# Recurrence outputs in PSUM tiles of their own, the block inverse issued a wave later, and row maxima turned by one product and one transfer

## The chip, the core and the metric

The kernel runs on one core of a Trainium2 chip. The metric is the time of one execution on the device in microseconds (us). Five engines work side by side, each through its own queue in a fixed order: TensorE (PE; its weight loads are shown apart as PEld), VectorE (DVE), ScalarE (ACT), GpSimd (POOL) and SyncE (SP, which here only issues DMAs).

## The reference

Two layers (`DEPTH = 2`) of a diffusion backbone over 256 context and 1024 latent tokens, model width 1024. Each layer scales and shifts the stream, makes one wide input projection, and feeds three groups of heads:

- A: six heads of 64 of a bidirectional recurrence (RWKV-7). Each head keeps a 64 x 64 state `S`; forward and backward scans run over context, then latent tokens.
- B: six query heads over two key heads, softmax attention over all keys.
- C: four heads of neighbourhood attention, 8 x 16 windows with a bias, plus all context keys.

Their gated outputs go through one output projection and a layer norm. The recurrence and the softmax are what the change touches:

```python
def _rwkv7_step(S, inp):
    r, w, k, v, kk, b = inp
    sa = jnp.einsum('bhvk,bhk->bhv', S, kk)
    S = S * w[:, :, None, :] - sa[..., None] * b[:, :, None, :] + v[..., None] * k[:, :, None, :]
    return S, jnp.einsum('bhvk,bhk->bhv', S, r)
...
        s = jnp.einsum('bqgrd,bsgd->bgrqs', qi, keys).astype(jnp.float32)
        p = jax.nn.softmax(s, axis=-1).astype(vals.dtype)
        return jnp.einsum('bgrqs,bsgd->bqgrd', p, vals)
```

## The kernel before

The program is written as tile code in Python; a scheduler that models the engines' times orders each engine's instructions when the program is built, taking the ready instruction that was written earliest. On the chip the order of each engine is then fixed: an instruction that waits holds up all that stand behind it on its engine.

**Layers.** A layer is `layer_proj` (projections, weights and activations split in a high and a low part, three products each, L203 to L205), `rwkv` (the recurrence, called in the middle of the projections by `mid()`), `attention` and `out_proj`. The recurrence is written ahead of the attention, so its instructions come first where both are ready, and attention fills what is left. Both overlap from 575 to 1160 us in layer 0 and from 1800 to 2385 us in layer 1; these two stretches are called the mixed stretches below.

**Recurrence.** 1280 tokens are cut into ten waves of 128, a wave into four steps of 32 tokens; the three head pairs and both directions of a step are computed together. `wave_chain` (L681 on) does a step: twelve products `rs` (L704) of the state with the keys; ACT copies them to `rsb` (L710); twelve products `sa` (L715) with the inverse block `tt`; ACT (three) and DVE (one) copy them into the state tile `x` (L721); twelve products `z` (L725) make the new state, which DVE scales into the next `x` (L730). The step's output, `out_step` (L742 to L744), is twelve products into `y`, which DVE copies to `yst`; it is put on the list `pend` and written into the next step, between `rs` and `rsb`. `rs`, `sa`, `z` and `y` are columns of one PSUM bank, the tile `ch`: `rs` and `sa` have columns 0 to 191, `z` 0 to 383, `y` 320 to 511. Only three state tiles `X` are there, so step s + 3 writes over the one that the output of step s reads.

**Preparation.** Each wave is prepared ahead by six stages: `p` (`wave_pre`: load, decay; it ends with `dc`, a copy of the decays on DVE, L575), `g` (`wave_gram`: products `gt` masked into `G`), `l` (`wave_low`: the diagonal blocks go out to `ls_d` in DRAM and come back turned as `lin`, L595 to L601), `i` (`wave_inv`: two DVE copies of `lin` to `nn`, L635 and L636, then 30 small DVE steps, and a round through DRAM to `di`), `k` (`wave_kt`: transposes), `m` (`wave_merge`: 192 small products `mg`, L675, that make `tt`). The small PSUM products of preparation (`psz`, `pcu`, `gt`, `kt`, `mg`, and `pso` of `out_block`) share two slots of the pool `pa`, tag `pp`. The main loop (L790 to L799) orders the stages of an iteration as `kpglmi`, so `i` of a wave is written right behind its `l`, ahead of the next wave's chain.

**Attention.** The heads are cut into 30 units (each of the ten heads has one for latent queries in each layer, and one for context queries in layer 0). A unit has two jobs of up to 512 queries. `pair_max` (L856) computes the scores a first time (`sm`, L867) and takes each query's maximum on DVE (L869 to L871; then `nm`, L874, one column of 128 queries). Each column is then turned into a row by a product with the identity (`mt`, L880, 180 of them, two PE instructions each), and ACT copies a job's row into row 64 of the query tile `q[1]` (L881). `pair_main` computes the scores again, turned (`st`: L936, and L937 which has row 64 among its 65 rows and so subtracts the maximum), exponentiates (ACT, L943) and multiplies with the values (L921). The maxima of a unit are interleaved with the main part of the unit before; the count `npc` in `attention` (L1076) paces them.

Of the kernel before, what the change touches and what calls it, by code (L numbers as in the profile page):

```python
# [8 lines left out]
F32 = mybir.dt.float32  # L9
# [34 lines left out]
def body(tc, a):  # L44
# [467 lines left out]
    def rwkv(l, lay):  # L512
# [10 lines left out]
        y = bank[:, 320:512].rearrange("p (c v) -> p c v", c=3)  # L523
# [22 lines left out]
        def wave_pre(w):  # L546
            dc = r2.tile([128, 2, 4, 3], F32, tag="dc", name="dc", bufs=4)
            prep[w] = dict(dc=dc, d=[], g=[])
            for d in range(2):
# [25 lines left out]
                nc.vector.tensor_copy(dc[:, d], lp[:, :, :, 32 * o:32 * o + 1].rearrange("p c j o -> p (j o) c"))  # L575
# [107 lines left out]
        def wave_chain(w):  # L683
# [5 lines left out]
            for j in range(4):  # L689
# [10 lines left out]
                for c in range(3):  # L700
                    for d in range(2):
                        for p in range(2):
                            q = QSA[d][p]
                            nc.tensor.matmul(out=rs[q:q + 32, c, :], lhsT=gs[d][:, jc[d], c, p, 0:32], rhs=x[:, d, c, p, :],  # L704
                                             start=True, stop=True, tile_position=(0, q))
                for f in pend:
                    f()
                pend.clear()
                rsb = r2.tile([128, 3, 64], F32, tag="rsb", name="rsb")
                nc.scalar.copy(rsb, rs)  # L710
# [26 lines left out]
        def out_step(w, j, x, jc, gs, yst):  # L737
            for c in range(3):
                for d in range(2):
                    for p in range(2):  # L740
                        q = QSA[d][p]
                        nc.tensor.matmul(out=y[q:q + 32, c, :], lhsT=gs[d][:, jc[d], c, p, 32:64], rhs=x[:, d, c, p, :],  # L742
                                         start=True, stop=True, tile_position=(0, q))
            nc.vector.tensor_copy(yst[:, j], y)  # L744
            if j == 3:
                for d in range(2):
                    for p in range(2):
                        q = QSA[d][p]
                        nc.sync.dma_start(out=y_d[d, 128 * w:128 * w + 128, :][:, 192 * p:192 * p + 192].rearrange("(j t) f -> t j f", t=32),
                                          in_=yst[q:q + 32].rearrange("t j c v -> t j (c v)"))  # L750
# [39 lines left out]
        for w in range(-3, NW):  # L790
            if w >= 0:
                wave_chain(w)
            for c in "kpglmi":
                v = w + (2 if c in "km" else 3)
# [13 lines left out]
    def attention(l):  # L808
# [47 lines left out]
        def pair_max(q, k, jobs, nq, bias):  # L856

            nm = ap2.tile([128, 8], F32, tag="nm", name="nm")
            for i, job in enumerate(jobs):
                q0 = job["q0"]  # L860
                for qt in range(nq // 128):
                    qc = q0 + 128 * qt
                    pcs = job["parts"](qt)
                    mx = ap2.tile([128, 4], F32, tag="mx", name="mx", bufs=4)
                    for n_, (c0, o, bcol) in enumerate(pcs):
                        sp_ = pst.tile([128, 512], F32, tag="sm", name="sm", bufs=2)
                        nc.tensor.matmul(out=sp_[:, :o], lhsT=q[0][:, qc:qc + 128], rhs=k[0][:, c0:c0 + o], start=True, stop=True)  # L867
                        if bcol is None:
                            nc.vector.tensor_reduce(out=mx[:, n_:n_ + 1], in_=sp_[:, :o], op=ALU.max, axis=AX.X)  # L869
                        else:  # L870
                            nc.vector.tensor_tensor_reduce(out=sp_[:, :o], in0=sp_[:, :o], in1=bias[0][:, bcol:bcol + o], scale=1.0, scalar=-3.0e38,  # L871
                                                           op0=ALU.add, op1=ALU.max, accum_out=mx[:, n_:n_ + 1])
                        if n_ == len(pcs) - 1:
                            nc.vector.tensor_reduce(out=nm[:, 4 * i + qt:4 * i + qt + 1], in_=mx[:, :len(pcs)], op=ALU.max, axis=AX.X, negate=True)  # L874
                        yield
            for i, job in enumerate(jobs):
                q0 = job["q0"]
                mt = pst.tile([128, 512], F32, tag="sm", name="mt", bufs=2)
                for qt in range(nq // 128):
                    nc.tensor.matmul(out=mt[64:65, 128 * qt:128 * qt + 128], lhsT=nm[:, 4 * i + qt:4 * i + qt + 1], rhs=ident, start=True, stop=True, tile_position=(0, 64))  # L880
                nc.scalar.copy(q[1][64:65, q0:q0 + nq], mt[64:65, :nq])  # L881
                yield
# [186 lines left out]
        while True:  # L1069
# [3 lines left out]
            if nxt is not None:  # L1073
                q, k, v, jobs, nq, och, bias = nxt
                mg = pair_max(q, k, jobs, nq, bias)
                npc = sum(len(j["parts"](t)) for j in jobs for t in range(nq // 128)) + 2  # L1076
# [315 lines left out]
```

## Time and profile before

| | |
|---|---|
| median of 3 runs | 2510.26 us (2495.68 to 2519.41) |
| the profiled execution's own time | 2503.84 us |
| its span, first to last instruction | 2502.0 us |
| granted TensorE clock over the span | 0.926 |
| busy: PE, DVE, ACT, POOL | 88%, 66%, 39%, 47% of the span |
| mixed stretch of layer 0 | 575 to 1160 us |
| mixed stretch of layer 1 | 1800 to 2385 us |

A row of the grouped instructions reads: line, engine, operation, output and inputs, shapes, count | busy time and mean duration | idle time of that engine just before them and what ended it. In the list of waits a row says who waited for whom, the total, how often and the longest. A row of the timeline has the start, the time until the last of the merged instructions ends, and the engine.

### The profile page before, as it was taken

The numbers are of one execution on the slowest core, as the hardware profiler recorded it, in microseconds if no ns is written. First come the engines' busy times: TensorE is split into PE (matmuls) and PEld (weight loads), VectorE is DVE, ScalarE is ACT, GpSimd is POOL, SyncE is SP. The second block draws the span as 40 slices with busy tenths as digits, with TensorE's granted clock in tenths as the row PEclk, the third lists the DMA queues.
The fourth block names the chain that finished last, engine by engine and source line by source line (L and its number), as shares of the span: only waits on it lengthen the run. The fifth ranks groups of instructions, "written<-read, shape, count | busy, mean of one in ns | idle before, by whom it ended". The sixth has DMA issues, their size and how long they took to land.

```text
span 2502.0 us, 57786 instructions
## 1 busy us (share of the span) xinstructions
PE 2204.5 (88%) x22616; PEld 1655.1 (66%) x22616; DVE 1660.7 (66%) x3183; ACT 978.7 (39%) x2074; POOL 1188.3 (47%) x1438
## 2 busy tenths in 40 slices
PE   6989999986878798999899999999868788989897
PEld 4777898764555555555797777787655555645497
DVE  5686524546887778676386795524478787777746
ACT  3333413333544344554234434223334434445522
POOL 3464426335564454453246356334456545545443
PEclk9999999997898899989999999999869989989899
DMA  7345335446555434452332455335555444432332
GB/s 278 111 158 167 109 92 127 114 108 142 120 123 115 109 93 106 125 156 60 99 100 90 138 166 184 104 88 130 143 113 126 92 105 107 96 81 66 122 113 93
DMA packets 448241, 298.17 MB, mean 119 GB/s; under 512 B 249600, under 2 KB 395880, under 8 KB 446944
## 3 DMA queue, kind: packets, MB, share of 16 engines
q1 hardware_dynamic: 439936, 281.71, 41.2%
q0 software_dynamic: 7392, 10.28, 1.5%
q8 instruction: 178, 2.92, 0.5%
q10 hardware_dynamic: 640, 2.49, 0.4%
q14 instruction: 95, 0.78, 0.1%
HBM read 198.37 MB, written 91.79 MB: 116 GB/s over the span
## 4 chain that ended last, share of the span: by engine, by line
PE 47%; DVE 21%; DMA 14%; issue 6%; ACT 5%; SPq 4%; POOL 3%; DVEq 0%; POOLq 0%; ACTq 0%
PE pj L203 5%; PE pj L204 5%; PE pj L205 5%; PE y L921 4%; DMA ls_d<-G 3%; PE sm L867 2%; PE st L936 2%; DVE mx L869 2%; DVE e L646 2%; DMA lin<-ls_d 2%; PE pj L1159 2%; PE st L937 2%; DVE G L616 2%; PE pj L1161 2%; PE pj L1160 2%
## 5 line engine op out<-in xcount | busy, mean ns | idle before, releaser
L204 PE MATMUL pj<-hlo,wh 128*128 128x512 f32 (+1 forms) x1072 | 403.0, 376 | 12.3 <-DVE hlo L480 7.2
L203 PE MATMUL pj<-hhi,wh 128*128 128x512 f32 (+1 forms) x1072 | 404.9, 380 | 7.4 <-ACT qr L348 4.7
L205 PE MATMUL pj<-hhi,wl 128*128 128x512 f32 (+1 forms) x1072 | 400.8, 375 | 0.0
L204 PEld LDWEIGHTS pj<-hlo,wh 128*128 128x128 f32 x1072 | 205.6, 192 | 54.9 <-DVE hlo L480 7.3
L169 POOL TENSOR_TENSOR wl<-wf,wh 128x512 fp32r<-128x512 f32 x104 | 142.2, 1371 | 209.3 <-ACT wh L168 194.6
L203 PEld LDWEIGHTS pj<-hhi,wh 128*128 128x128 f32 x1072 | 205.0, 192 | 52.8 <-issue 7.0
L943 ACT ACTIVATE pt<-st 128x512 f32<-128x512 f32 (+1 forms) x292 | 165.2, 582 | 174.7 <-PE st L937 171.4
L205 PEld LDWEIGHTS pj<-hhi,wl 128*128 128x128 f32 x1072 | 205.5, 192 | 37.7 <-issue 3.1
L869 DVE TENSOR_REDUCE mx<-sm 128x1 f32<-128x512 f32 (+1 forms) x372 | 198.9, 553 | 39.2 <-PE sm L867 37.5
L921 PE MATMUL y<-pt,v 128*64 128x256 f32 (+1 forms) x1392 | 221.2, 406 | 2.7 <-ACT pt L943 2.3
L936 PE MATMUL st<-q,k 128*128 128x512 f32 (+3 forms) x376 | 168.0, 451 | 22.6 <-DVE am L110 6.5
L867 PE MATMUL sm<-k,q 128*128 128x256 f32 (+2 forms) x436 | 169.7, 432 | 19.5 <-DVE mx L869 7.8
L1159 PE MATMUL pj<-yh,wh 128*128 128x256 f32 x576 | 160.0, 294 | 11.8 <-ACT yh L1133 10.7
L1160 PE MATMUL pj<-yl,wh 128*128 128x256 f32 x576 | 164.7, 289 | 0.8 <-POOL yl L1134 0.8
L1161 PE MATMUL pj<-yh,wl 128*128 128x256 f32 x576 | 163.2, 288 | 0.0
L921 PEld LDWEIGHTS y<-pt,v 128*64 128x64 f32 x1392 | 97.1, 146 | 96.3 <-issue 66.3
L950 POOL TENSOR_TENSOR acc<-acc,pt 128x512 f32<-128x512 f32 x80 | 104.5, 1306 | 116.5 <-ACT pt L943 109.9
L937 PE MATMUL st<-q,k 65*128 65x512 f32 (+3 forms) x376 | 151.3, 406 | 1.4 <-ACT q L881 1.3
L867 PEld LDWEIGHTS sm<-k,q 128*128 128x128 f32 x436 | 84.8, 210 | 81.6 <-issue 21.0
L616 DVE TENSOR_TENSOR G<-gt,msk 64x192 f32<-64x192 f32 (+1 forms) x320 | 110.5, 345 | 39.6 <-PE gt L611 28.7
L699 POOL MEMSET X<- 32x192 f32 x320 | 82.9, 259 | 93.2 <-PE ch L742 68.8
L630 ACT COPY S<-kt 64x192 f32<-64x192 f32 x320 | 100.4, 314 | 55.4 <-PE ch L725 28.7
(276 smaller groups left out, 5137.2 us busy)
## 6 DMA issues: line engine op xcount, KB each, us to landing
wf<-win SPq DMA_DIRECT2D x104, 256.0 KB
wm<-wmod SPq DMA_DIRECT2D x32, 512.0 KB
yf<-yg_d SPq DMA_DIRECT2D x72, 128.0 KB
wt<-wm SPq DMA_DIRECT2D x8, 1024.0 KB
gate_d<-o SPq DMA_DIRECT2D x32, 256.0 KB
wf<-wout SPq DMA_DIRECT2D x16, 512.0 KB
ldkk<-rw_d SPq DMA_DIRECT2D x40, 192.0 KB
ldkd<-rw_d SPq DMA_DIRECT2D x40, 192.0 KB
```

The costliest lines, as they stand in the source:

```text
L203: nc.tensor.matmul(out=ps[:, :n], lhsT=wh, rhs=hhi[:, k, t0:t0 + n], start=(k == 0), stop=False)
L204: nc.tensor.matmul(out=ps[:, :n], lhsT=wh, rhs=hlo[:, k, t0:t0 + n], start=False, stop=False)
L205: nc.tensor.matmul(out=ps[:, :n], lhsT=wl, rhs=hhi[:, k, t0:t0 + n], start=False, stop=(k == KT - 1))
L867: nc.tensor.matmul(out=sp_[:, :o], lhsT=q[0][:, qc:qc + 128], rhs=k[0][:, c0:c0 + o], start=True, stop=True)
L869: nc.vector.tensor_reduce(out=mx[:, n_:n_ + 1], in_=sp_[:, :o], op=ALU.max, axis=AX.X)
L921: mm = nc.tensor.matmul(out=y[64 * i:64 * i + 64, a0:a1], lhsT=v[:, t, :], rhs=pt[:, p0:p0 + a1 - a0], start=start, stop=stop and at == le ...
L936: nc.tensor.matmul(out=o, lhsT=k[0][:, 128 * t:128 * t + 128], rhs=q[0][:, qa:qb], start=True, stop=False)
L937: mm = nc.tensor.matmul(out=o, lhsT=k[1][0:65, 128 * t:128 * t + 128], rhs=q[1][0:65, qa:qb], start=False, stop=True)
L943: nc.scalar.activation(out=pt[:, :w], in_=sp_[:, :w], func=AF.Exp)
L1159: nc.tensor.matmul(out=p_, lhsT=wh[m][:, k], rhs=yh, start=(x_ == 0), stop=False)
L1160: nc.tensor.matmul(out=p_, lhsT=wh[m][:, k], rhs=yl, start=False, stop=False)
L1161: nc.tensor.matmul(out=p_, lhsT=wl[m][:, k], rhs=yh, start=False, stop=(x_ == KT - 1))
```

## The change

Four edits:

1. `out_step` takes its output from a tile `py` of the pool `pa` (tag `pp`) and no longer from a strip of the bank `ch`; ACT and not DVE copies it to `yst`; and `rsb` is written ahead of the outputs that are on the list `pend`.
2. The copy `dc` goes from DVE to ACT.
3. The stages of an iteration stand as `ikpglm`, and `i` works on the wave w + 2 where it worked on w + 3: the inverse of a wave is written one iteration later than its `l`, ahead of the other stages of that iteration.
4. The maxima of a whole unit are reduced at once (`nm`, 8 columns or 2), turned by one product to 8 rows of 128 (`mt`), copied by ACT to `mr`, and flattened by a DMA that POOL issues into row 64 of `q[1]`; the separate reductions, the 180 products and the 60 copies go. `npc` is one less.

```diff
-        y = bank[:, 320:512].rearrange("p (c v) -> p c v", c=3)
...
-                nc.vector.tensor_copy(dc[:, d], lp[:, :, :, 32 * o:32 * o + 1].rearrange("p c j o -> p (j o) c"))
+                nc.scalar.copy(dc[:, d], lp[:, :, :, 32 * o:32 * o + 1].rearrange("p c j o -> p (j o) c"))
...
+                rsb = r2.tile([128, 3, 64], F32, tag="rsb", name="rsb")
+                nc.scalar.copy(rsb, rs)
                 for f in pend:
                     f()
                 pend.clear()
-                rsb = r2.tile([128, 3, 64], F32, tag="rsb", name="rsb")
-                nc.scalar.copy(rsb, rs)
...
         def out_step(w, j, x, jc, gs, yst):
+            y = pa.tile([128, 3, 64], F32, tag="pp", name="py")
...
-            nc.vector.tensor_copy(yst[:, j], y)
+            nc.scalar.copy(yst[:, j], y)
...
-            for c in "kpglmi":
-                v = w + (2 if c in "km" else 3)
+            for c in "ikpglm":
+                v = w + (2 if c in "ikm" else 3)
...
-                        if n_ == len(pcs) - 1:
-                            nc.vector.tensor_reduce(out=nm[:, 4 * i + qt:4 * i + qt + 1], in_=mx[:, :len(pcs)], op=ALU.max, axis=AX.X, negate=True)
                         yield
-            for i, job in enumerate(jobs):
-                q0 = job["q0"]
-                mt = pst.tile([128, 512], F32, tag="sm", name="mt", bufs=2)
-                for qt in range(nq // 128):
-                    nc.tensor.matmul(out=mt[64:65, 128 * qt:128 * qt + 128], lhsT=nm[:, 4 * i + qt:4 * i + qt + 1], rhs=ident, start=True, stop=True, tile_position=(0, 64))
-                nc.scalar.copy(q[1][64:65, q0:q0 + nq], mt[64:65, :nq])
-                yield
+            nc.vector.tensor_reduce(out=nm[:, :n], in_=mx[:, :n, :len(pcs)], op=ALU.max, axis=AX.X, negate=True)
+            mt = pst.tile([128, 512], F32, tag="sm", name="mt", bufs=2)
+            nc.tensor.matmul(out=mt[:n, 0:128], lhsT=nm[:, :n], rhs=ident, start=True, stop=True)
+            mr = ap2.tile([8, 128], F32R, tag="mr", name="mr")
+            nc.scalar.copy(mr[:n], mt[:n, 0:128])
+            q0 = jobs[0]["q0"]
+            nc.gpsimd.dma_start(out=q[1][64:65, q0:q0 + 128 * n].rearrange("o (n t) -> o n t", t=128), in_=mr[:n])
+            yield
...
-                npc = sum(len(j["parts"](t)) for j in jobs for t in range(nq // 128)) + 2
+                npc = sum(len(j["parts"](t)) for j in jobs for t in range(nq // 128)) + 1
```

The scheduler orders the whole program anew. Two places show it.

The first is PE in layer 1, at the fourth neighbourhood unit and the fifth wave of the recurrence (wave 4, counted from 0). Before, the turning products `mt` stand in lots of seven and one (each product is two PE instructions), and the `st` product that reads row 64 (L937) stands two rows behind the first lot; `ch` with `tt` is `sa`, with `S` it is `z`, and `pcu` is preparation.

```order
7629 L867 MATMUL sm<-k_24678,q_24686 128x256
7630 L880 MATMUL mt<-c_ident,nm 1x128 x7
7631 L568 MATMUL pcu<-tri,th 128x128 x3
7632 L937 MATMUL st<-q_24687,k_24679 128x512
7633 L725 MATMUL ch<-X_17549,S_17536 64x64 x6
7634 L725 MATMUL ch<-X_17549,S_17537 64x64 x6
7635 L880 MATMUL mt<-c_ident,nm 1x128
```

In the changed program, one product `mt`, and behind it outputs `py` of two steps, then the `rs` (L703) and `sa` (L714) of a step, and only then the first L938, which reads row 64.

```order
7692 L878 MATMUL mt<-c_ident,nm 8x128
7693 L937 MATMUL st<-q_24455,k_24447 128x512
7694 L742 MATMUL py<-X_17350,G_17332 32x64 x2
...
7700 L742 MATMUL py<-X_17348,G_17332 32x64 x2
...
7706 L937 MATMUL st<-q_24455,k_24447 128x512
7707 L703 MATMUL ch<-X_17349,G_17332 32x64 x2
...
7713 L714 MATMUL ch<-rsb,tt 32x64 x12
7714 L938 MATMUL st<-q_24456,k_24448 128x512 x2
```

Seven products went, and the reader of row 64 moved from two rows behind the turning product to behind 24 outputs, two `st` products and a step's `rs` and `sa`.

The outputs moved too. Before, the output of a step (here the one in X_17549) stands right behind the `rs` of the next (X_17550):

```order
7646 L704 MATMUL ch<-X_17550,G_17532 32x64 x2
7647 L704 MATMUL ch<-X_17550,G_17533 32x64 x2
7648 L742 MATMUL ch<-X_17549,G_17532 32x64 x2
7649 L742 MATMUL ch<-X_17549,G_17533 32x64 x2
```

In the changed program, for the same wave, the output of its first step (X_17349) stands behind the second lot of merge products of the next wave:

```order
7680 L922 MATMUL y<-pt_24608,v 64x128
7681 L674 MATMUL mg<-di 32x32 x48
7682 L742 MATMUL py<-X_17349,G_17332 32x64 x2
7683 L742 MATMUL py<-X_17349,G_17333 32x64 x2
```

So an output waits for a slot that preparation holds: those of the first three steps of this wave (X_17349, X_17350, X_17348) stand in one lot, and the fourth step, which writes over X_17349 (row 7707), stands behind them.

The second place is DVE in layer 1, at the two copies `nn<-lin` that start the inverse of the sixth wave. Before, the first stands two rows behind a step's new state (L730) and ahead of the masking of `gt` (L616); the second comes eleven rows later (row 1918).

```order
1905 L730 TENSOR_TENSOR X_17550<-ch,dc 64x6x64 x2
1906 L955 TENSOR_TENSOR acc_24469<-acc_24469,pt_24625 128x256
1907 L635 COPY nn<-lin 64x256
1908 L955 TENSOR_TENSOR acc_24468<-acc_24468,pt_24625 128x128
1909 L744 COPY yst<-ch 128x192
1910 L616 TENSOR_TENSOR G_17535<-gt,msk 64x3x64 x8
```

In the changed program, for the same wave, the first stands seven rows behind the new state of the same step (L729) and behind that masking (L615); the second is row 1713.

```order
1693 L729 TENSOR_TENSOR X_17350<-ch,dc 64x6x64 x2
1694 L873 ISA sm,mx<-sm,bs 128x384
1695 L873 ISA mx 128x1
1696 L871 TENSOR_REDUCE mx<-sm 128x1
1697 L1003 TENSOR_TENSOR gtl<-ys,tb 128x4x16x8
1698 L615 TENSOR_TENSOR G_17335<-gt,msk 64x3x64 x8
1699 L946 TENSOR_TENSOR pt_24347<-st,bt 128x384
1700 L634 COPY nn<-lin 64x256
```

The start of the inverse has moved by a few rows within the same step, not by a wave, and the copy `yst` is no longer among DVE's rows.

More of the change, by code (lines that the diff above doesn't have):

```diff
@@ L858, in pair_max @@
             nm = ap2.tile([128, 8], F32, tag="nm", name="nm")
+            n = 2 * nq // 128
+            mx = ap2.tile([128, 8, 3], F32, tag="mx", name="mx")
             for i, job in enumerate(jobs):
@@ L863, in pair_max @@
                     pcs = job["parts"](qt)
-                    mx = ap2.tile([128, 4], F32, tag="mx", name="mx", bufs=4)
+                    u = nq // 128 * i + qt
                     for n_, (c0, o, bcol) in enumerate(pcs):
@@ L868, in pair_max @@
                         if bcol is None:
-                            nc.vector.tensor_reduce(out=mx[:, n_:n_ + 1], in_=sp_[:, :o], op=ALU.max, axis=AX.X)
+                            nc.vector.tensor_reduce(out=mx[:, u, n_:n_ + 1], in_=sp_[:, :o], op=ALU.max, axis=AX.X)
                         else:
                             nc.vector.tensor_tensor_reduce(out=sp_[:, :o], in0=sp_[:, :o], in1=bias[0][:, bcol:bcol + o], scale=1.0, scalar=-3.0e38,
-                                                           op0=ALU.add, op1=ALU.max, accum_out=mx[:, n_:n_ + 1])
-                        if n_ == len(pcs) - 1:
-                            nc.vector.tensor_reduce(out=nm[:, 4 * i + qt:4 * i + qt + 1], in_=mx[:, :len(pcs)], op=ALU.max, axis=AX.X, negate=True)
+                                                           op0=ALU.add, op1=ALU.max, accum_out=mx[:, u, n_:n_ + 1])
                         yield
-            for i, job in enumerate(jobs):
-                q0 = job["q0"]
-                mt = pst.tile([128, 512], F32, tag="sm", name="mt", bufs=2)
-                for qt in range(nq // 128):
-                    nc.tensor.matmul(out=mt[64:65, 128 * qt:128 * qt + 128], lhsT=nm[:, 4 * i + qt:4 * i + qt + 1], rhs=ident, start=True, stop=True, tile_position=(0, 64))
-                nc.scalar.copy(q[1][64:65, q0:q0 + nq], mt[64:65, :nq])
-                yield
+            nc.vector.tensor_reduce(out=nm[:, :n], in_=mx[:, :n, :len(pcs)], op=ALU.max, axis=AX.X, negate=True)
[6 more added lines that the diff above has]
+            yield
         def pair_main(q, k, v, jobs, nq, och, bias, end):
```

## Prediction

> **What bounds the kernel now.** I read the page's totals first, then the windows by stage, then the list of waits of PE.
>
> ```profile
> span 2502.0 us, 57786 instructions
> ...
> PE 2204.5 (88%) x22616; PEld 1655.1 (66%) x22616; DVE 1660.7 (66%) x3183; ACT 978.7 (39%) x2074; POOL 1188.3 (47%) x1438
> ...
> PE 47%; DVE 21%; DMA 14%; issue 6%; ACT 5%; SPq 4%; POOL 3%; DVEq 0%; POOLq 0%; ACTq 0%
> ```
>
> PE is busy 88% of the span and has the largest share of the chain that ended last; DVE is next, with 21% (525 us). The two mixed stretches, where recurrence and attention share the engines, hold all that the change touches, but for the first waves' preparation:
>
> ```profile
> core 0: us, PE busy (x) PEld busy (x) DVE busy (x) ACT busy (x) POOL busy (x), PEclk, DMA share, GB/s
> 575.00:1160.00 585.00, 494.55 (x7098) 317.59 (x7097) 450.15 (x1118) 273.50 (x645) 304.41 (x379) 0.88 0.47 117
> 1800.00:2385.00 585.00, 488.70 (x7017) 317.35 (x7017) 457.16 (x1080) 268.98 (x608) 310.40 (x390) 0.87 0.44 106
> sum 1170.00, PE 983.25 PEld 634.95 DVE 907.32 ACT 542.48 POOL 614.81; mean PE 491.62 PEld 317.47 DVE 453.66 ACT 271.24 POOL 307.41
> ```
>
> In 1170 us PE is busy 983 and idle 187; DVE is busy 907 (78%), ACT only 542. What PE waits for in its idle time:
>
> ```profile
> PE kt L626 <- DVE tt L680: 20.2, 9, 5.1
> PE ch L725 <- DVE X L721: 19.1, 10, 4.5
> PE ch L715 <- ACT rsb L710: 17.2, 9, 5.3
> PE mg L675 <- DVE di L678: 10.6, 3, 7.9
> PE mt L880 <- DVE mx L869: 9.9, 6, 7.3
> PE pcu L568 <- DVE th L565: 9.2, 7, 3.0
> ...
> PE mg L675 <- issue: 7.1, 7, 2.2
> ```
>
> The releaser is mostly DVE: PE's work and DVE's lateness set the mixed stretches. A recurrence step shows how:
>
> ```profile
> 910.66 0.54 PE L704 MATMUL ch<-X,G 128*32 128x64 f32 x24
> ...
> 911.02 0.52 PE L742 MATMUL ch<-X,G 128*32 128x64 f32 x24
> ...
> 911.87 1.29 DVE L869 TENSOR_REDUCE mx<-sm 128x1 f32<-128x512 f32 x2
> ...
> 913.07 0.35 DVE L744 COPY yst<-ch 128x192 f32<-128x192 f32 x1
> ...
> 913.51 0.32 ACT L710 COPY rsb<-ch 128x192 f32<-128x192 f32 x1 [0.25 <-DVE yst L744]
> ```
>
> `rs` is done at 911.20, but ACT copies it at 913.51: the copy waits for `yst` on DVE, and that one stood behind two maxima. A step loses 2.3 us here. The groups that the terms below use:
>
> ```profile
> L880 PE MATMUL mt<-c_ident,nm 128*1 128x128 f32 x360 | 56.7, 300 | 17.8 <-DVE mx L869 9.9 <-DVE mx L871 6.0 <-DVE nm L874 1.9
> ...
> L715 PE MATMUL ch<-rsb,tt 32*32 32x64 f32 x1920 | 51.6, 238 | 18.7 <-ACT rsb L710 18.4
> ...
> L575 DVE COPY dc<-lp 128x12 f32<-128x12 f32 x40 | 28.5, 711 | 56.8 <-ACT lp L573 56.6
> ...
> L881 ACT CAST q<-mt 1x512 fp32r<-1x512 f32 (+1 forms) x60 | 27.7, 470 | 26.4 <-PE mt L880 25.8
> ...
> L874 DVE TENSOR_REDUCE nm<-mx 128x1 f32<-128x3 f32 (+2 forms) x180 | 26.5, 147 | 2.0
> L710 ACT COPY rsb<-ch 128x192 f32<-128x192 f32 x80 | 25.5, 319 | 106.8 <-DVE yst L744 94.3 <-PE ch L704 5.8 <-DVE G L616 2.3
> L744 DVE COPY yst<-ch 128x192 f32<-128x192 f32 x72 | 25.3, 351 | 16.9 <-PE ch L742 15.7 <-DMA stg<-q_d 0.5
> ...
> L636 DVE COPY nn<-lin 64x256 f32<-64x256 f32 x20 | 9.4, 469 | 73.5 <-DMA lin<-ls_d 73.4
> ```
>
> **The change part by part.**
>
> *Products of the maxima (A, B).* 180 products of two PE instructions become 30, so 300 instructions go. What one costs in PE's stream:
>
> ```profile
> 928.60 0.82 PE L880 MATMUL mt<-c_ident,nm 128*1 128x128 f32 x6
> 929.35 0.66 PE L996 MATMUL tb<-c_ident,rb 128*128 128x128 f32 x4
> ...
> 935.99 0.38 PE L880 MATMUL mt<-c_ident,nm 128*1 128x128 f32 x2
> 936.30 0.50 PE L867 MATMUL sm<-k,q 128*128 128x512 f32 x1
> ```
>
> Six take 0.75 us until the next instruction starts (0.125 each), a lone pair 0.31 (0.155). 300 x 0.125 to 0.155 is 37 to 46 us; I take 42 (0.14). It lies on the engine that is the bound: A = -42. Ahead of these products PE sat idle 17.8 us, since they come as soon as the last maximum may be there; thirty products in place of sixty lots leave half: B = -9, from 0 to -18.
>
> *DVE's work (C).* `yst` (25.3) and `dc` (28.5, much of it spent blocked, as 12 elements a row need no 711 ns) leave DVE, and 150 of 180 small reductions (26.5 x 150/180 = 22.1): 76 us, 4.6% of DVE's 1661. The chain has 525 us of DVE; 4.6% of that is C = -24. It ends at 0 if other rows stand ready to take its place on the chain, at -76 if each microsecond passes through. ACT takes over 72 `yst` at the 0.32 of `rsb`, the same shape (23 us), and 40 `dc` at no more than that (13), and gives back most of the 27.7 of the 60 casts. ACT is idle 628 us of 1170 in the mixed stretches, so this is taken at nothing; without that cover it would be some 15 us.
>
> *`rsb` ahead of the outputs (D).* ACT was idle 94.3 us for `yst` ahead of `rsb`, but PE itself sat idle only 18.4 of it ahead of `sa`, since attention filled the rest. D = -12, from 0 to -18. What is late next is the copy of `sa` by DVE (L721), in the list above with 19.1.
>
> *Outputs in slots of `pa`.* The order of PE (the change, above) shows that the output now stands behind `mg` of the next wave, and the fourth step behind the lot of outputs. The products are the same in number, and attention stands ahead in that gap, so I take nothing; the upper bound is what PE already waits for preparation in the list (`kt` 20.2, `mg` 10.6 and 7.1, `pcu` 9.2), paid once more: +47.
>
> *The inverse a wave later.* DVE stood 73.4 us for `lin`, 3.7 a wave. The order shows the start of the inverse moved by a few rows in the same step, so the wait for `lin` can stay; all of it gone would be worth at most its share of the chain, 73.4 x 21% = 15. On the other side the merge now follows its inverse's own round through DRAM within an iteration; the nearest price is that same 73.4. The order leaves two to three steps between the two, so I take nothing, from -15 to +73.
>
> *The flattening transfer (E).* New in each unit: between the cast and the first L938 lies a DMA that POOL issues. The only POOL transfers inside the mixed stretches are `zs`; POOL's queue also holds the sums of the exponentials:
>
> ```profile
> zs<-zs_d POOLq DMA_DIRECT2D x40, 49.0 KB, 2.3
> ```
> ```profile
> L950 POOL TENSOR_TENSOR acc<-acc,pt 128x512 f32<-128x512 f32 x80 | 104.5, 1306 | 116.5 <-ACT pt L943 109.9 <-PE ch L742 3.9 <-DVE mx L869 1.9
> ```
>
> Issue to landing takes 2.3 us; the shorter cast gives back some 0.2, so 2.1 a unit, and 30 units make 64. Where the issue also stands behind a sum that waits for ACT, 116.5/80 = 1.5 more: 3.6 a unit, 109. Queued behind L938 on PE are the recurrence's products, and DVE and ACT wait for those. At the place shown in the order, 24 outputs (1.04 by the 0.52 for 24 instructions above), `rs` and `sa` (0.54 and about as much) and two `st` products cover some 3 us: the bare transfer, but not the queue. I take E = +25, a quarter of the upper end; from 0 to +109.
>
> The Trainium skill speaks against such a transfer: by SBUF — State Buffer, section "SBUF: two separate sides", POOL cannot write a DMA's descriptors while DVE runs an instruction in a mode that takes their shared port, and a transfer of 620 ns then takes 3100. By that page's figures E would be larger by 30 x 2.5 = 74 at the most, an estimate. The trace bears it out little: the `zs` transfers land in 2.3 us in the median with DVE 78% busy.
>
> The sum: 2502 - 42 - 9 - 24 - 12 + 25 = 2440. Around the span lie 1.8 us (2503.84 against 2502.0), and the median of the runs is 6.4 above the profiled run: 2448 us, 2.5% faster.
>
> **The rivals.**
>
> *All of DVE's relief passes through, and the transfer is hidden.* -42 - 18 - 76 - 18 gives 2348, with the 8.2 around it 2356. For it: DVE ends most of PE's waits. Against: attention fills most waits already.
>
> *Only the products count.* DVE's relief and the early `rsb` move waits and don't shorten them, the transfer costs its 25: 2502 - 42 + 25 + 8 = 2493. For it: of ACT's 94 us for `yst`, PE felt 18.
>
> *The outputs' tiles tie the recurrence to the preparation, so the change does not free it.* D is lost and the 47 are paid: 2502 - 42 - 9 - 24 + 25 + 47 + 8 = 2507. For it: the order above. Against: attention stands in the gap, and PE has the same work.
>
> *The transfer gates each unit: slower.* L938 stands still in all 30 units for 3.6 us: 2502 - 42 - 24 - 12 + 109 + 8 = 2541. It decides from 2.6 us a unit (78/30), where the gains are used up; at 3.4 the time is 1% longer. For it: L938 waits for nothing but this, and the POOL queue ahead of it waits for ACT. Against: the order has put work between. The Trainium skill's page named above would make this the likelier end.
>
> **How the numbers follow.** Chances: the forecast 0.53, all passes through 0.10, only the products 0.18, slots 0.06, the transfer gates 0.13. A difference of 1% is about what a measurement of this kernel can tell from none, as its runs spread by 0.5% to either side. Faster by over 1% (under 2485) takes the forecast's case but for an edge of 0.03, the second case, and a third of the third: 0.66. Within 1%: that edge, the rest of the third, the slots, and 0.02 of the transfer: 0.23. Slower: 0.11. The range of 8 in 10 goes from 2385, which leaves half of the case where all passes through, to 2515, which takes in the two cases without a difference and leaves the transfer's.
>
> **What would show it.** In the profile of the changed kernel: PE's group of `mt` at 60 instructions and about 9 us; DVE's busy time some 75 us lower; ACT's idle time ahead of `rsb` put down to PE and no longer to DVE; PE's idle time in the mixed stretches down from 187 towards 140. L938 waiting for the transfer should total about 25 us; over 78 the fourth rival holds. If DVE still stands for `lin` some 60 us or more, the inverse has not moved, as I read the order. The forecast is wrong if PE's idle time in the mixed stretches has not fallen, or if `kt`, `mg` and `pcu` wait twice as long as before.

## The result: no faster

The changed kernel takes 2517.8 us (median of 20 runs, 2503.0 to 2532.9), the kernel before 2505.5 us beside it (20 runs, 2493.7 to 2520.7): the ratio on record is 1.0069, with a 95% interval from 1.0049 to 1.0088 (the two medians alone give 1.0049). The forecast was 2448 us. These are the page's totals of the changed kernel:

```profile
span 2507.8 us, 57143 instructions
...
PE 2204.9 (88%) x22316; PEld 1652.6 (66%) x22316; DVE 1624.1 (65%) x2921; ACT 981.2 (39%) x2156; POOL 1199.2 (48%) x1468
```

PE has 300 instructions fewer and is busy for 2204.9 us, where it was 2204.5. That is the riddle: the work went, its time stayed. DVE's busy time fell by 37 us. The groups that the forecast spoke of (line, engine, operation, shapes, count | busy, mean ns | idle time before and what ended it):

```profile
L938 PE MATMUL st<-q,k 65*128 65x512 f32 (+3 forms) x376 | 150.5, 410 | 6.0 <-DMA q<-mr 6.0
L703 PE MATMUL ch<-X,G 128*32 128x64 f32 x1920 | 65.8, 242 | 34.7 <-DVE X L729 18.9 <-POOL X L698 4.9 <-DMA X<-vt_d 4.8
L742 PE MATMUL py<-X,G 128*32 128x64 f32 x1728 | 58.4, 244 | 23.3 <-DVE tt L679 19.5 <-issue 3.7
L714 PE MATMUL ch<-rsb,tt 32*32 32x64 f32 x1920 | 49.0, 235 | 4.4 <-ACT rsb L706 4.4
L706 ACT COPY rsb<-ch 128x192 f32<-128x192 f32 x80 | 25.4, 317 | 83.1 <-PE ch L703 72.2 <-DVE tmp L643 5.9 <-DVE acc L951 1.9
L744 ACT COPY yst<-py 128x192 f32<-128x192 f32 x72 | 22.8, 319 | 65.2 <-PE py L742 61.7 <-DMA lin<-ls_d 2.9
L878 PE MATMUL mt<-c_ident,nm 128*8 128x128 f32 (+1 forms) x60 | 12.3, 290 | 7.8 <-DVE nm L876 7.8
L634 DVE COPY nn<-lin 64x256 f32<-64x256 f32 x20 | 10.5, 526 | 20.3 <-DMA lin<-ls_d 20.1
L635 DVE COPY nn<-lin 64x256 f32<-64x256 f32 x20 | 6.2, 312 | 60.8 <-DMA lin<-ls_d 60.7
L574 ACT COPY dc<-lp 128x12 f32<-128x12 f32 x40 | 8.6, 215 | 0.3
```

Each edit did at its own place what it says: `rsb` waits for PE and no longer for `yst`; PE waits 4.4 us for it (18.4 before); the transfer holds PE for 6.0 us in all. New is the wait of the outputs for the merged block `tt`, 19.5 us. The windows of the two mixed stretches, and the list of what PE waits for from 575 to 2385 us:

```profile
core 0: us, PE busy (x) PEld busy (x) DVE busy (x) ACT busy (x) POOL busy (x), PEclk, DMA share, GB/s
575.00:1160.00 585.00, 510.32 (x6902) 322.59 (x6903) 433.80 (x990) 274.49 (x677) 300.43 (x391) 0.86 0.47 113
...
1800.00:2385.00 585.00, 483.07 (x6729) 311.34 (x6726) 424.62 (x947) 262.12 (x627) 295.80 (x377) 0.85 0.39 95
```
```profile
PE sm L869 <- DVE mx L871: 21.0, 27, 2.6
PE pcu L567 <- DVE th L564: 17.8, 11, 5.8
PE ch L703 <- DVE X L729: 14.9, 9, 4.0
PE pso L780 <- DVE yo L776: 12.8, 4, 5.2
PE py L742 <- DVE tt L679: 11.8, 5, 3.8
PE ch L724 <- DVE X L720: 8.1, 4, 4.5
...
PE mg L674 <- DVE di L677: 4.7, 3, 2.4
...
PE kt L625 <- DVE tt L679: 3.9, 3, 2.3
```

The waits changed their names: `kt`, `mg` and `z` less; `pcu`, `pso`, the outputs and above all `sm` more (21.0 us for the maxima `mx`, where the same row had 7.8). And the column that the forecast passed over has moved: the granted clock fell from 0.88 and 0.87 to 0.86 and 0.85, over the span from 0.926 to 0.912.

**What the clock does here.** The records of the granted clock have two values, 1 and 0.5, and change on a grid of 3.41 us. At half clock PE's work takes about 1.8 times as long: in the changed kernel, from one start to the next, an `sm` product of 128x512 takes 335 ns at full clock and 594 at half (medians of 163 and 29), an L1160 product of `out_proj` 120 and 213. Counted over the profiled executions of 19 kernels of this case (the two and all those below but `twice`), window by window of this grid from the first record of the clock on:

| a window at full clock, PE busy in it | windows | the next is at half clock |
|---|---|---|
| under 0.5 | 768 | 733 (95%) |
| 0.5 to 0.6 | 324 | 178 (55%) |
| 0.6 to 0.7 | 423 | 61 (14%) |
| 0.7 and more | 10041 | 39 (0.4%) |

From a window at half clock the next one is at half clock again in 881 of 929 cases if PE was busy less than 0.9 of it, and in 329 of 1273 if more. So PE need not stand still for a window to lose its clock; half idle is enough, and it mostly takes a nearly full window to get it back. The Trainium skill, TensorE: Matmul & The Clock Gate, section "Part 1: The HAM clock gate (the "warmup" mystery)", has the same two speeds and a window of about 3.4 us, but says that the clock falls after an idle window; the counts differ from it there.

How this looks at the place of the change: the third lot of turning products in layer 1, with the next score that reads row 64, in the timeline of PE of the changed kernel and of the kernel before, and the windows of the grid around them, six and five:

```profile
1945.95 0.28 PE L878 MATMUL mt<-c_ident,nm 128*8 128x128 f32 x1
1946.07 0.27 PE L878 MATMUL mt<-c_ident,nm 128*8 128x128 f32 x1
...
1957.14 1.20 PE L938 MATMUL st<-q,k 65*128 65x512 f32 x2
```
```profile
1934.03 1.87 PE L880 MATMUL mt<-c_ident,nm 128*1 128x128 f32 x8 [5.14 <-DVE mx L871]
...
1936.62 1.87 PE L880 MATMUL mt<-c_ident,nm 128*1 128x128 f32 x8
1938.42 0.58 PE L937 MATMUL st<-q,k 65*128 65x512 f32 x1
```
```profile
core 0: us, PE busy (x) PEld busy (x) DVE busy (x) ACT busy (x) POOL busy (x), PEclk, DMA share, GB/s
1942.49:1945.90 3.41, 3.41 (x47) 2.48 (x45) 2.10 (x9) 0.87 (x2) 0.74 (x2) 0.50 0.75 276
1945.90:1949.32 3.42, 2.61 (x54) 1.74 (x57) 2.58 (x9) 3.19 (x9) 3.10 (x7) 1.00 0.15 33
1949.32:1952.73 3.41, 1.25 (x27) 0.62 (x15) 0.00 (x0) 3.26 (x11) 3.33 (x4) 1.00 0.48 112
1952.73:1956.14 3.41, 2.32 (x27) 2.20 (x28) 2.09 (x7) 1.11 (x3) 0.74 (x3) 0.50 0.56 66
1956.14:1959.56 3.42, 3.42 (x35) 2.61 (x34) 2.41 (x5) 2.01 (x6) 1.47 (x2) 0.50 0.82 189
1959.56:1962.97 3.41, 3.41 (x43) 2.33 (x44) 2.69 (x5) 2.12 (x7) 3.26 (x4) 1.00 0.79 220
```
```profile
core 0: us, PE busy (x) PEld busy (x) DVE busy (x) ACT busy (x) POOL busy (x), PEclk, DMA share, GB/s
1931.79:1935.21 3.42, 1.18 (x6) 0.72 (x7) 2.50 (x9) 0.32 (x1) 3.10 (x8) 0.50 0.50 115
1935.21:1938.62 3.41, 3.41 (x37) 1.81 (x34) 0.34 (x1) 1.61 (x5) 1.34 (x3) 0.50 1.01 259
1938.62:1942.03 3.41, 2.85 (x77) 2.01 (x79) 2.02 (x5) 1.68 (x3) 0.00 (x0) 1.00 1.09 220
1942.03:1945.45 3.42, 3.42 (x93) 2.36 (x91) 2.87 (x9) 2.55 (x5) 2.38 (x5) 1.00 0.91 137
1945.45:1948.86 3.41, 2.47 (x72) 1.65 (x71) 1.89 (x8) 1.95 (x5) 2.25 (x2) 1.00 0.36 91
```

After the single product (two PE instructions) no score that reads row 64 stands in PE's order for 11 us; one window is busy for 1.25 us of 3.41 and the two that follow run at half clock. In the kernel before, the products run at half clock, as PE had been idle ahead of them; the clock is back behind them, a score that reads row 64 starts at once, and the clock holds. This is one pair of places; over all units the clock is at half for 7%, 8% and 13% of the time from 0 to 4, 4 to 8 and 8 to 12 us after the last turning product begun in the kernel before, and for 15%, 30% and 44% in the changed one (23 and 22 lots of products; a lot ends where none begins for 15 us).

**The balance.** A profiled execution is then made of three parts: PE idle; PE's work, counted at full clock (its busy time less half of its busy time at half clock); and what the half clock adds to it (that half; it takes the factor as 2, and with the 1.8 measured this part would be a ninth smaller). For the kernel before 297.5 + 2055.3 + 149.2 = 2502.0, for the changed one 302.9 + 2027.9 + 177.0 = 2507.8. Work fell by 27, and the clock gave 28 back.

### The profile page after: what moved, and what is told of

Its sections match the earlier page's. It is cut to its first block, busy times and chain, and to the rows that moved or that the text cites. A ratio compares the mean times of both kernels' runs of the same rounds, so it can differ in the third digit from the quotient of the medians.

```text
span 2507.8 us, 57143 instructions
## 1 busy us (share of the span) xinstructions
PE 2204.9 (88%) x22316; PEld 1652.6 (66%) x22316; DVE 1624.1 (65%) x2921; ACT 981.2 (39%) x2156; POOL 1199.2 (48%) x1468
## 4 chain that ended last, share of the span: by engine, by line
PE 25%; DVE 13%; DMA 9%; issue 4%; ACT 3%; POOL 2%; SPq 1%; POOLq 0%; DVEq 0%; ACTq 0%
PE y L922 3%; DMA yf<-yg_d 2%; PE st L937 2%; PE sm L869 2%; PE pj L204 2%; PE pj L203 2%; PE pj L205 2%; DMA ls_d<-G 1%; PE st L938 1%; PE pj L1160 1%; PE pj L1162 1%; PE pj L1161 1%; PE ch L724 1%; DVE G L615 1%; DVE acc L951 1%
## 5 line engine op out<-in xcount | busy, mean ns | idle before, releaser
L937 PE MATMUL st<-q,k 128*128 128x512 f32 (+3 forms) x376 | 173.8, 467 | 25.0 <-DVE gtl L999 7.1
L1160 PE MATMUL pj<-yh,wh 128*128 128x256 f32 x576 | 161.8, 293 | 12.1 <-ACT yh L1134 10.0
L938 PE MATMUL st<-q,k 65*128 65x512 f32 (+3 forms) x376 | 150.5, 410 | 6.0 <-DMA q<-mr 6.0
L615 DVE TENSOR_TENSOR G<-gt,msk 64x192 f32<-64x192 f32 (+1 forms) x320 | 110.4, 345 | 38.3 <-PE gt L610 27.1
L937 PEld LDWEIGHTS st<-q,k 128*128 128x128 f32 x376 | 77.6, 207 | 79.1 <-ACT pt L944 18.4
```

Source lines behind the costliest of these rows:

```text
L937: nc.tensor.matmul(out=o, lhsT=k[0][:, 128 * t:128 * t + 128], rhs=q[0][:, qa:qb], start=True, stop=False)
L938: mm = nc.tensor.matmul(out=o, lhsT=k[1][0:65, 128 * t:128 * t + 128], rhs=q[1][0:65, qa:qb], start=False, stop=True)
L1160: nc.tensor.matmul(out=p_, lhsT=wh[m][:, k], rhs=yh, start=(x_ == 0), stop=False)
```

## The experiments

Eighteen kernels, told nearly in the order in which they ran. The balance of each stands in one table; "products" are the instructions of `mt` on PE, and all times but the ratio are of one profiled execution, in us.

| kernel | products | ratio to before (95% interval) | PE idle | half-clock busy | half clock adds | work |
|---|---|---|---|---|---|---|
| before | 360 | 1 | 298 | 298 | 149 | 2055 |
| null_b | 360 | 1.0010 (0.9985 to 1.0036) | 319 | 260 | 130 | 2058 |
| null_b2 | 360 | 1.0042 (1.0005 to 1.0080) | 294 | 294 | 147 | 2058 |
| acts | 360 | 0.9942 (0.9915 to 0.9968) | 296 | 284 | 142 | 2061 |
| no_y_mx | 360 | 1.0021 (0.9986 to 1.0056) | 307 | 292 | 146 | 2061 |
| no_mx | 360 | 0.9893 (0.9869 to 0.9917) | 264 | 273 | 137 | 2077 |
| turn8 | 360 | 1.0060 (1.0039 to 1.0080) | 309 | 289 | 145 | 2060 |
| mx_only | 60 | 0.9993 (0.9977 to 1.0010) | 316 | 358 | 179 | 2007 |
| after | 60 | 1.0069 (1.0049 to 1.0088) | 303 | 354 | 177 | 2028 |
| null_a | 60 | 0.9917 (0.9887 to 0.9948) | 292 | 345 | 172 | 2035 |
| null_a2 | 60 | 1.0066 (1.0039 to 1.0093) | 305 | 390 | 195 | 2027 |
| early | 60 | 1.0094 (1.0064 to 1.0123) | 307 | 383 | 192 | 2022 |
| no_y | 60 | 0.9924 (0.9901 to 0.9948) | 300 | 308 | 154 | 2027 |
| no_inv | 60 | 0.9966 (0.9946 to 0.9987) | 285 | 357 | 179 | 2028 |
| fill | 280 | 1.0000 (0.9976 to 1.0024) | 295 | 291 | 146 | 2059 |
| null_a_fill | 280 | 0.9946 (0.9918 to 0.9974) | 293 | 283 | 142 | 2057 |
| no_y_fill | 280 | 0.9992 (0.9966 to 1.0018) | 294 | 335 | 167 | 2042 |
| fill2 | 560 | 1.0102 (1.0068 to 1.0135) | 292 | 317 | 159 | 2081 |
| b_double | 720 | 1.0109 (1.0070 to 1.0149) | 285 | 333 | 167 | 2088 |

**The fourth edit alone** (`pair_max` of the changed kernel in the kernel before; mx_only).

> The kernel before with the fourth edit alone (maxima of a unit reduced at once, turned by one product, flattened by the transfer). The profile of the changed kernel has the turning products at 9.4 us where they were 51.0, and L938 waits only 6.0 us for the transfer. Theory 1 (the output tiles and the stage order cost what the maxima gain): this edit alone keeps its gain, -41.6 - 10 + 6 = about -45, so 2460 us, ratio 0.982. Rival (PE's work taken away comes back as slower clock and as waits, whichever edit takes it away): 2495 to 2510, ratio 0.996 to 1.002.

2505.2 us, 0.9993: the rival's number. The edit that takes 39 us of products from PE gains nothing, also without the others.

**The outputs back in the bank** (no_y).

```diff
+        y = bank[:, 320:512].rearrange("p (c v) -> p c v", c=3)
...
-            y = pa.tile([128, 3, 64], F32, tag="pp", name="py")
```

> The changed kernel with the output y back in columns 320 to 511 of the bank ch; ACT still copies it, rsb still stands ahead. Theory 1a (the slots of pa tie the recurrence to the preparation; rs and the outputs cost PE 28 us more there, and at four wave ends the recurrence halts some 45 us): the gain comes back, about 2460 us, ratio 0.982. Theory 1b (the stage order is the cause): no more than 10 us, 2508 to 2518, ratio 1.001 to 1.005. Rival (the clock takes any gain): the same as 1b.

2488.2 us, 0.9924: better than the changed kernel by 30 us by the medians and 36 by the ratios, more than theory 1b allows (10) and short of what 1a asks (58).

**The old order of the stages** (no_inv).

```diff
-            for c in "ikpglm":
-                v = w + (2 if c in "ikm" else 3)
+            for c in "kpglmi":
+                v = w + (2 if c in "km" else 3)
```

> The changed kernel with the stages in the old order kpglmi and the inverse in its old place. In the changed kernel PE stands 19.5 us ahead of the outputs for the merged block tt, which no output waited for before. Theory 1b (the inverse a wave later makes the merge late): those waits go and the gain of some 45 to 60 us comes back, 2460 to 2475 us, ratio 0.982 to 0.988. Theory 1a (slots): the outputs still wait in line with the preparation, 2505 to 2520, ratio 1.000 to 1.006.

2501.8 us, 0.9966: better than the changed kernel by 16 us by the medians and 26 by the ratios, about half of what theory 1b asks at the most.

**Without the maxima's edit** (`pair_max` and `npc` of the kernel before in the changed one; no_mx).

> The changed kernel with the maxima as before (180 reductions and products, 60 casts, no transfer). Theory 1 (the maxima's edit gains some 45 us and the others lose 57): 2518 + 45 = 2563 us, ratio 1.022. Rival (PE's work taken away comes back as slower clock): 2510 to 2530 us, ratio 1.002 to 1.010.

2482.4 us, 0.9893. Both expectations fall: the kernel is faster with the 300 products than without. Taken alone, each of three edits now seemed to cost 1.0 to 1.8% in the changed kernel, more than there is to explain. I first took the longer way from a unit's last maximum to its first score for the cause, since L938 comes later behind the products than before.

**The transfer twice** (twice).

```diff
+            mr2 = ap2.tile([8, 128], F32R, tag="mr2", name="mr2")
+            nc.gpsimd.dma_start(out=mr2[:n], in_=mr[:n])
-            nc.gpsimd.dma_start(out=q[1][64:65, ...], in_=mr[:n])
+            nc.gpsimd.dma_start(out=q[1][64:65, ...], in_=mr2[:n])
```

> The changed kernel with the transfer made twice in a row (first to a second tile of the same shape, then to row 64). In the runs so far the changed kernel without the maxima's edit takes 2482 us, with it 2518, though L938 waits only 6 us for the transfer in it. Theory 2 (the way from the last maximum to the first score of the unit, 3.5 us longer with the transfer, holds up attention, whose end sets the end in layer 1, and PE does thin recurrence work at half clock in the meantime): a second transfer costs about as much again, 2518 + 35 = 2553 us, ratio 1.018. Rival (clock and density of PE: the removed products kept PE busy): no change, 2510 to 2525, ratio 1.001 to 1.007.

2834.8 us, 1.1335, nine times the price expected. The timelines of POOL (the last transfer of a unit) and of PE (the next score of attention) show why this is no price of a transfer:

```profile
759.17 0.52 POOL L884 DMA_DIRECT2D q<-mr  x1 [0.99 <-DMA inv_d<-ee]
```
```profile
1084.11 0.69 PE L939 MATMUL st<-q,k 128*128 128x384 f32 x1
```

In PE's order the score stands 325 us behind the issue, behind all that was left of the recurrence (whose last `z` starts at 1037), and the same happens once in layer 1. The scheduler put it there when it built the program; PE does not wait for the transfer. This kernel is left out of the table, as it has another course of work altogether. It says nothing for theory 2.

**The maxima an iteration earlier** (early).

```diff
-                    while mg is not None and done < npc * (i + 1) // nit:
+                    while mg is not None and done < min(npc, npc * (i + 1) // (nit - 1)):
```

> The changed kernel with the maxima of a unit paced so that they are written one iteration of the main part of the unit before earlier; the transfer has that iteration to land in. Theory 2 (the longer way from maximum to score holds up attention): the 35 us come back, about 2480 us, ratio 0.990, if the earlier maxima cost nothing themselves. Rival (clock and density of PE): no change, 2510 to 2525, ratio 1.001 to 1.007.

2521.7 us, 1.0094, where theory 2 expected 0.990. But the edit did not do what it was meant to: PE still waits 5.8 us for the transfer (6.0 in the changed kernel), and from the last turning product of a lot to the next score that reads row 64 it is 5.9 us in the median (5.8). By these figures it gave the transfer no more time, so theory 2 is not tested by it.

**One reduction, but the products as before** (turn8).

```diff
-            nc.tensor.matmul(out=mt[:n, 0:128], lhsT=nm[:, :n], rhs=ident, start=True, stop=True)
...
+                for qt in range(nq // 128):
+                    u = nq // 128 * i + qt
+                    nc.tensor.matmul(out=mt[64:65, 128 * qt:128 * qt + 128], lhsT=nm[:, u:u + 1], rhs=ident, start=True, stop=True, tile_position=(0, 64))
+                nc.scalar.copy(q[1][64:65, q0:q0 + nq], mt[64:65, :nq])
```

> The changed kernel with the transfer and the one product taken out: the maxima are still reduced at once for a unit, but turned column by column (300 products more) and copied by ACT into row 64 as before. Theory 2 (the way through the transfer): 2482 us, ratio 0.990, as without the whole edit. Rival 2a (the reduction at once, which holds all products back until the last maximum of the unit, is the cause and not the transfer): 2518 plus the products' 42 less what clock takes, 2518 to 2560, ratio 1.004 to 1.021.

2514.7 us, 1.0060, as the changed kernel: without a transfer and with 300 more instructions on PE. The half-clock busy time is 289 us, where the changed kernel has 354. The number of theory 2 is missed, but two things changed at once: a price of the transfer can hide behind the price of the 300 instructions, so the transfer is not cleared by this kernel.

**Idle products** (fill; the product is made six times, two times in the small units, into the same place).

```diff
-            nc.tensor.matmul(out=mt[:n, 0:128], lhsT=nm[:, :n], rhs=ident, start=True, stop=True)
+            for _ in range(6 if n == 8 else 2):
+                nc.tensor.matmul(out=mt[:n, 0:128], lhsT=nm[:, :n], rhs=ident, start=True, stop=True)
```

> The changed kernel with the one product of a unit made six times over (two times in the small units) into the same place, which puts back about 270 of the 300 instructions on PE, 38 us, and leaves the transfer. Rival (clock and density of PE: PE filled keeps its clock): no change or a gain, 2500 to 2520, ratio 0.998 to 1.005. Theory 2 (the way from maximum to score): the products lengthen that way by 0.7 us more a unit and take PE's time, 2518 + 20 to 40 = 2538 to 2558, ratio 1.013 to 1.021.

2500.5 us, 1.0000: 0.7% faster than the changed kernel with 220 instructions more. The page's totals, and the product's group:

```profile
span 2498.8 us, 57577 instructions
...
PE 2204.3 (88%) x22536; PEld 1654.9 (66%) x22536; DVE 1626.1 (65%) x2921; ACT 983.0 (39%) x2156; POOL 1198.0 (48%) x1468
```
```profile
L879 PE MATMUL mt<-c_ident,nm 128*8 128x128 f32 (+1 forms) x280 | 45.1, 314 | 2.1 <-DVE nm L876 2.1
```

PE's busy time is 2204 once more. The granted clock is back at 0.928.

**An edit without work** (null_b in the kernel before, null_a in the changed one; null_b2 and null_a2 have 2 for the 1).

```diff
-                    if n_it >= 20 and n_it % 3 == 0:
+                    if n_it >= 20 and n_it % 3 == 1:
```

> The kernel before with an edit that takes nothing away and adds nothing: the pieces of the modulation that are spread over the attention's iterations are taken at every third iteration counted one later. Only the order that the scheduler builds from it changes (some 4000 rows of PE's list). Theory 3 (a new order moves the time by up to 1% either way, and what was put down to single edits is partly this): off the kernel before by more than 5 us either way, ratio under 0.998 or over 1.002. Theory 4 (each edit has its own price): the time of before, ratio 0.998 to 1.002.

> The changed kernel with the same edit that takes nothing away and adds nothing (the modulation's pieces one iteration later). Theory 3 (a new order moves the time by up to 1% either way): off the changed kernel's ratio 1.007 by more than 0.003 either way. Theory 4 (each edit has its own price): ratio 1.004 to 1.010.

> The kernel before with the modulation's pieces two iterations later (nothing added or taken away). If orders scatter here too: off 1.000 by more than 0.004, and PE's busy time at half clock still 260 to 298 us. If the order of before is steadier than that of the changed kernel: 0.997 to 1.003.

> The changed kernel, with the modulation's pieces two iterations later (nothing added or taken away). If its orders scatter by 1.5% as the first two did: anywhere from 0.990 to 1.010, and PE's busy time at half clock 308 to 383 us as in the others without the products. If the first result of this kind was the exception: 1.004 to 1.010.

null_b has the time of before, 1.0010; null_b2 1.0042; null_a 0.9917, 1.5% off the changed kernel; null_a2 1.0066, its time. A new order of the same work can move this kernel by 1.5%. So one kernel with one part undone tells nothing of a part's price below that, and the mean over orders has to speak: 1.0017 for the changed kernel (1.0069, 0.9917, 1.0066), 1.0017 for the kernel before (1, 1.0010, 1.0042). The profiled execution of null_a (span 2499.6) was the slowest of its eight, whose median is 2481.9; its row of the table is to be read so.

**Neither the output tiles nor the maxima** (no_y_mx), and **only the copies on ACT and `rsb` first** (acts, the kernel before with three edits of the diff: `dc` and `yst` on ACT, `rsb` ahead of `pend`).

> The changed kernel without its first and its fourth edit's main parts: y stays in the bank ch and the maxima stay as before; yst and dc on ACT, rsb ahead of the outputs and the inverse a wave later remain. Theory 4 (prices that add up: y in the slots 1.4%, the maxima 1.8%): 1.0069 - 0.0145 - 0.0176 = 0.975, 2442 us. Theory 3 (orders scatter): not under 0.985, anywhere from 0.985 to 1.005.

> The kernel before with yst and dc on ACT and rsb ahead of the outputs, nothing else. Terms C (without the reductions) and D of the forecast: -24 x 54/76 - 12 = -29 us, ratio 0.988. Theory 4 agrees within 0.004 of the kernel without the output tiles and maxima (0.975 to 0.990). Theory 3: anywhere from 0.985 to 1.005.

no_y_mx has 1.0021, where adding up gives 0.975: theory 4 falls. acts has 0.9942, 16 us (8 to 21 by its interval), with PE's idle time as before (296). The 29 us expected of it lie outside. The gain is not larger than what a new order can do.

**Idle products in two other orders, more of them, and each product of before twice** (null_a_fill, no_y_fill; fill2 has 12 and 4 for 6 and 2; b_double has `for _ in range(2):` ahead of the product at L880).

> The changed kernel with the modulation's pieces one iteration later (ratio 0.9917), and in addition the one product of a unit made six times over. Theory 5 (at the place of the removed products PE is too thinly busy to hold its clock; filled there, it holds it): PE's busy time at half clock falls from 345 us to 260 to 305, and the 38 us of added products cost at most 10 us, ratio 0.985 to 0.996. Rival (the products cost PE their time, the run with filled products was faster by its order alone): half-clock time stays within 20 us of 345, ratio 1.003 to 1.010.

> The changed kernel with y in the bank ch (ratio 0.9924, PE busy at half clock 308 us), and in addition the one product of a unit made six times over. Theory 5: half-clock time 260 to 300 us, time within 10 us of the kernel without the fill, ratio 0.988 to 0.997. Rival: half-clock time about 308, 38 us more, ratio about 1.007.

> The changed kernel with the one product of a unit made twelve times over (four times in the small units): some 580 instructions and 80 us on PE more than the changed kernel. Theory 5: once the clock holds, further work costs its time; half-clock time 260 to 300 us, ratio 1.000 (six times over) + 40/2505 = 1.016, from 1.008 to 1.020. Rival (the products cost PE their time from the first): 1.007 + 80/2505 = 1.039. Rival (PE is not the bound there at all): 1.000 to 1.007.

> The kernel before with each turning product made twice: 360 instructions, 51 us, more on PE. Theory 5: half-clock time is at its floor of 260 to 298 us already, so the work costs most of its time: 30 to 51 us, ratio 1.012 to 1.020. Rival (PE's work at this place is not what the end waits for, and its removal could gain nothing for that reason): ratio 0.996 to 1.005.

In null_a_fill the half-clock time falls from 345 to 283 us, as theory 5 expects, and 220 instructions more cost 0.3%. In no_y_fill it does not: 335 us after 308, and 0.7% more time, which lies short of the rival's 1.007 and above theory 5's 0.997. Over the three pairs the ratio moves by -0.7, +0.3 and +0.7%, 0.1% in the mean, for 220 instructions that at 0.14 us would cost 31 us or 1.2%. Where the products are there already, more of them cost: fill2 is 1.0% above fill for 280 more, b_double 1.1% above before for 360 more (26 and 27 us, where 0.14 us each gives 39 and 50). Their half-clock time, 317 and 333 us, lies above the 260 to 300 and 260 to 298 expected.

## Why the forecast was wrong, by its steps

**A failed, and with it the forecast.** The 300 instructions left PE as told (51.0 to 9.4 us from each start to the next one, -41.6 for the -42 of the term). The step that failed is the sentence "It lies on the engine that is the bound: A = -42". It took PE's busy time for a store of work at one speed, and the sum has no term for the clock. In the terms of the balance the forecast took 62 us off the span, and 6 came on top: 42 of these 68 us are A (work -27 and clock +28, where -42 was forecast), 25 are PE's idle time (+5, where B, C, D and E together gave -20). The table shows what happens instead: the seven kernels with 360 products have a half-clock loss of 130 to 149 us, mean 142; the seven with 60 have 154 to 195, mean 178; no value of the one group lies in the other. The means of work are 2061 and 2025, of PE's idle time 298 and 301. Work -36, clock +36, idle +3: the removal is worth nothing, and the mean ratios of the two groups are 0.9995 and 1.0004. The balance alone does not tell whether the half clock held up the end or filled time in which PE would have stood waiting; that added products cost about half of their time (fill2, b_double) says that PE's work at this place reaches the end at least in part.

Where the clock is lost can be counted in the traces. In the first 12 us after the last turning product of each lot begins, PE's half-clock busy time is 19 to 41 us in the seven kernels with 360 products (mean 27) and 57 to 108 in the seven with 60 (mean 80). In the first 24 us the means are 73 and 149, and in all the rest of the span 212 and 208. So the whole difference lies right behind the turning products.

Which part of the fourth edit loses it stays open. One reading is that the missing products no longer fill PE there. Idle products bring the half-clock time of the profiled execution down in two orders (354 to 291 and 345 to 283) and not in a third (308 to 335); the granted clock over all runs of these kernels rises clearly in the first alone (0.912 to 0.927, 0.921 to 0.925, 0.917 to 0.918). And in those 12 us the time only goes from 66, 63 and 57 us to 54, 56 and 47, above each of the seven kernels with 360 products; most of the fall in the two orders lies elsewhere, where this reading does not explain it. The other reading is the longer way through the transfer: from the last turning product of a lot to the next score that reads row 64 it is 1.1 to 1.5 us in the median in the seven kernels with 360 products, 3.5 to 6.7 in the seven with 60, and 2.9 to 4.6 in the three with idle products. turn8, which has no transfer, has 22 us of half-clock time in the 12 us and a way of 1.3. Both readings may hold; no kernel shortens the way and leaves the products out.

**B** was right at its place: the idle time ahead of `mt` went from 17.8 to 7.8. PE's idle time in all did not fall.

**C** was mis-sized and did not pass. The three rows went (75.5 us), but the durations of all DVE rows together fell by 62 (by output tile `acc` grew by 14, `kb` by 6, `ee` by 5; `e` fell by 13), and DVE's busy time, which counts rows that overlap once, by 37. PE's idle time is 264 to 309 us (mean 296) in the fourteen kernels of the table that have `yst` and `dc` on ACT, and 285 to 319 (mean 302) in the five that have not: 6 us, where C and D together gave 36. That other DVE rows stood ready to take the place of those that left fits this, but is not shown.

**D** was right at its place (18.4 to 4.4) and no gain of it stands out in the sum: PE now stands 18.9 us for X ahead of `rs` and 19.5 for `tt` ahead of the outputs.

**Output tiles at nothing.** The halts exist: the fourth step of some waves starts 45 to 56 us after the third (waves 3, 8 and 18 of the 20 of both layers), where before the longest gap of two steps was 27, but for the first step of each layer. But their price does not stand out: the output tiles cost 1.4% between no_y and after, 0.1% between no_y_fill and fill, and gain 1.3% between no_y_mx and no_mx. The rival of the slots had nearly the time that came (2507) and not the reason.

**Inverse at nothing** was right as the order was read: DVE still stands 80.8 us for `lin` (86.2 before), above the 60 that the forecast named.

**E = +25** was too high at its place: 6.0 us of waiting. Whether the longer way costs more by the clock, as told under A, is open. The transfers land as fast as those of `zs`, here in the list of DMA issues (KB each, median us to landing) of the changed kernel:

```profile
zs<-zs_d POOLq DMA_DIRECT2D x40, 49.0 KB, 2.9
q<-mr POOLq DMA_DIRECT2D x20, 4.0 KB, 2.4
q<-mr POOLq DMA_DIRECT2D x10, 1.0 KB, 3.5
```

The rival of the transfer falls as it was stated, with L938 standing still 3.6 us in each unit. The 74 us more that the forecast worked out from the Trainium skill, SBUF — State Buffer, section "SBUF: two separate sides", are not borne out either, with DVE busy 65% of the span.

PE's idle time in the mixed stretches went from 187 to 177, not to 140, and its busy time there rose by 10 with 484 instructions fewer: by the forecast's own sign, little freed, and slower. The other sign was mixed: `kt` and `mg` fell, `pcu` went from 9.2 to 17.8. The range ended at 2515, 3 us under the result; it had no term for the clock and none for the order.

## What to carry to other kernels

Before costing the removal of PE work, count PE's busy share by windows of the clock's grid at that place: where it is near one half, taking work away can cost as much clock as it saves. Closing the idle gaps first, or placing useful work there, is the advice that follows; no kernel here tests it. Time two or three builds that differ only in order before a part of a change is given a price; here one null edit was worth 1.5%, more than the change. no_mx (0.9893) and null_a (0.9917) beat both kernels, but the kernel before by no more than an order does.

## What was not expected of the hardware

The half clock adds 130 to 195 us to PE's busy time in the kernels of the table (taken as a factor of 2), 5 to 8% of the span, though PE is busy 87 to 89% of it. Windows that are only half idle are enough for it. And the same program runs from 2483.4 to 2515.8 us on one chip (30 runs of before), 1.3%; no cause of that was tested.
